# Latent attention: values stationary, two heads on one output tile, one maximum and exp over 1024 keys, output made transposed

## The chip, the cores and the metric

The kernel is one program on one core of a Trainium2 chip. Its five engines, TensorE (PE in the profile), VectorE (DVE), ScalarE (ACT), GpSimd (POOL) and SyncE (SP, which issues almost all DMAs here), work through queues of their own, each in the order in which the program was laid down, and wait for each other by semaphores. The metric is the device time of one execution in microseconds (us).

## The reference

Two transformer blocks over 1024 tokens of width 1024. The first mixes two branches on the same normed input, latent attention and a bidirectional RWKV scan, gates them, projects the sum and adds it to the input; then come a mixture of experts and a second block. The change touches latent attention alone:

```python
def attend(blk):
    qn, qr = blk
    s = (jnp.einsum('bqhd,bkhd->bhqk', qn, k_nope)
         + jnp.einsum('bqhd,bkd->bhqk', qr, k_rope))
    p = jax.nn.softmax(s.astype(jnp.float32) * scale, axis=-1).astype(v.dtype)
    return jnp.einsum('bhqk,bkhd->bqhd', p, v)
```

There are 8 heads, 64 + 32 columns for queries and keys, 64 for values, 1024 keys for each of 1024 queries, without a mask. The RWKV branch works on 4 pairs of heads: `prep` makes what needs no running state, `inverse` inverts a small triangular matrix per chunk of 64 tokens, `rwkv_chain` carries the state over 16 chunks, `finish` does the group norm.

## The kernel before

`branches` (L1964) lays down, in this order, the input projection with RWKV's work hooked into it, and then `mla` (L784), the latent attention. A list scheduler then sets the order on each engine from its own estimate of durations and from when buffers come free, so `mla` is interleaved with what is left of RWKV when the projection ends: the preps of the third and fourth head pair, `inverse` of the second to fourth, and most of the chain.

RWKV's path. `prep` (four calls per head pair; two directions, two halves) and `inverse` use memory of their own, the pool `prep`, and two PSUM banks `pw`, taken in turn. `pair(j)` lays down one prep of pair j, then `inverse(j-1)` and the chain of pair j-1, then the other three preps. `inverse` (L641) loads blocks, does 31 dependent substitution steps on VectorE (L653 and the sum behind it, ending with the copy L657), writes them out, and then joins the blocks of four units with two rounds of small products each (L671, copy L674, L676, sum L679). In a prep, L581 follows the first tanh, L583 is the scan, L608 and L609 make block diagonals, L551 is the product and L558 and L559 its masked copies. `inverse(3)` is the last user of the pool `prep`, which is then closed.

Latent attention. `mla` loads the compressed keys and queries (zk, L792; zq, L794), scales them, and makes for each pair of heads the keys and values (`keys`, L819) and for each head and half of the tokens the rotated queries (`queries`, L845). Then for each head, for each of 8 row blocks b of 128 queries and each half q of the keys:
- `score`: three float32r products into one bank S (two buffers), the row maximum on VectorE (L879), its scaling (L881), exp with a running sum on ScalarE (L883);
- `flip`: four transposes on TensorE (L889), then a copy on VectorE for q = 0 (L894), on ScalarE for q = 1 (L892);
- `values`: four products with the transposed block as the stationary operand and 64 columns of V moving (L904), 128 queries on the output partitions.

The three are one step apart: scores of step n, transposes of n-1, values of n-2. Behind a head the two halves are brought to a common maximum and divided (L930 to L938), and behind each pair the output is transposed (L943) and written (L946) to om, which the next stage, `branch_out`, reads. A float32 product is two instructions in the profile, a float32r product or a transpose one.

Memory. Pools are stacked; one that is opened on the bytes of a closed pool waits for those that used them. The tiles of `mla`'s pool take 97,728 bytes a partition, from address 18,432 to 116,160, where the projection's operands had been. The lowest tile of the pool `prep` (xn0, used by `inverse`) begins at 119,360. PSUM has eight banks, all used here: pc two, pw two, S two, pt one, pj one.

Of the kernel before, what the change touches and what calls it, by code (L numbers as in the profile page):

```python
# [7 lines left out]
F32 = mybir.dt.float32  # L8
# [31 lines left out]


def _chunks(w):
    """[..., K, N] -> [..., N/512 * K/512, 128, 2048]: chunks of 4 k-blocks by 512 columns, k fastest."""
    K, N = w.shape[-2:]
    n = w.ndim - 2
    w = w.reshape(*w.shape[:-2], K // 512, 4, 128, N // 512, 512)
    o = list(range(n)) + [n + x for x in (3, 0, 2, 1, 4)]
    return np.ascontiguousarray(w.transpose(o)).reshape(*w.shape[:n], -1, 128, 2048)


def _constants():
    """Constants of the branches, and those of the whole program."""
# [138 lines left out]
# ---------------------------------------------------------------- device program  # L191

class Prog:
# [3 lines left out]
    def consts(self, pool, temp):  # L197
        """pool: for the whole program; temp: for the branches."""
# [17 lines left out]
    def keep(self, keep, dram):  # L216
        """Scratch memory, and the small tiles that several phases use."""
# [37 lines left out]
    def slots(self, table, n, base):  # L255
        """What marks the rows in table [128, 8, n, 6]: the row of its block plus base, the block and zero."""
# [5 lines left out]
    def thirds(self, table, x):  # L262
        """x in three bfloat16 parts that add up to it exactly, to table[..., 3:6]; x is overwritten."""
# [7 lines left out]
    def iota8(self, pool):  # L271
        """The slots (from 1), each eight times."""
# [15 lines left out]
    def order(self, later, first):  # L288
        """`later` is issued behind `first` on their engine: one accumulation at a time in a bank."""
# [3 lines left out]
    def rsqrt(self, pool, out, v, n):  # L293
        """out = v ** -0.5 by Newton steps; out, v: [128, n]."""
# [16 lines left out]
    def rsqrt1(self, pool, out, v):  # L311
        """The same for one column where ScalarE has its square root at hand."""
# [9 lines left out]
def s1(P, hpool, wpool, psum):  # L322
    """Reads x, normalises it and leaves its transpose, split, in hT (hi, lo)."""
# [18 lines left out]
def z_tile(P, spool, psum, hT, m, use):  # L342
    """z^T rows of column tile m of w_in; use(s, ps): the PSUM tile of the tokens s."""
# [15 lines left out]
def phase_a(P, zpool, spool, psum, hT, after=lambda j: None):  # L359
    """z^T = (h @ w_in)^T tile by tile; what later phases need goes to scratch memory."""  # L360
# [81 lines left out]
class Rwkv:  # L442
    """The RWKV branch: a head pair (two heads on 128 partitions) and half of the tokens at a time."""
# [13 lines left out]
    def own(self, dram, pool, psw):  # L457
        """Memory for prep alone."""
# [33 lines left out]
    def stats(self, src, scale, u=None):  # L492
        """[128 (h, ch), 512] -> sums over ch per (token, head): [128 t, 8 = (block, h)] times scale."""
# [7 lines left out]
    def spread(self, st, u=None):  # L501
        """[128 t, 8 = (block, h)] -> [128 (h, ch), 512] in PSUM."""
# [8 lines left out]
    def keys(self, p, g):  # L511
        """Normalised kk of head pair p, negated, to scratch memory."""
# [12 lines left out]
    def flip(self, p, d, g, m, x):  # L525
        """x [128 (h, ch), 512 tokens], transposed per head, to part m of the scratch memory."""
# [10 lines left out]
    def diag(self, i, f):  # L537
        """Block diagonal buffer i, written by f(destination, rows) for each head."""
# [6 lines left out]
    def gram(self, lb, AR, da, mask, dr):  # L545
        """lb^T [A | R] of every chunk (partition: the index of lb), under causal masks."""
# [14 lines left out]
    def prep(self, p, d, g):  # L561
        """Chunks 8 g to 8 g + 7 of head pair p in direction d: all that needs no running state, to memory."""
# [119 lines left out]
    def finish(self, p, g, u=None):  # L682
        """Group norm, bonus and gate of head pair p; half of o_rwkv^T of the pair."""
# [33 lines left out]
def rwkv_chain(P, pool, psum, p):  # L717
    """The running states of head pair p in both directions over the chunks; leaves y^T in scratch memory."""
# [5 lines left out]
    def mm(ps, terms):  # L724
        # one accumulation group per bank: only its first product clears the bank
# [58 lines left out]
def mla(P, dram, pool, psum):  # L784
    """Latent attention; leaves o_mla^T (four tiles [128, T]) in scratch memory."""
# [9 lines left out]
    for z, w, n in ((zk, 1, 2), (zq, 0, 3)):  # L795
        for q in range(2):
# [5 lines left out]
            rb = pool.tile([128, 512], F32, name="ot", bufs=1)  # L802
# [5 lines left out]
    for q in range(2):  # L808
        s = slice(512 * q, 512 * q + 512)
        kp = pool.tile([128, 512], F32, name="ot", bufs=1)  # L810
# [6 lines left out]
    def keys(pr):  # L817
        """Keys and values of head pair pr."""
# [26 lines left out]
    def queries(h, q):  # L845
        """Rotated queries of head h, half q of the tokens."""
# [5 lines left out]
        qh, ql = (pool.tile([128, 512], F32R, name=n, bufs=2) for n in ("qh", "ql"))  # L852
# [7 lines left out]
    Vn, nq = keys(0), queries(0, 0)  # L860
    for h in range(8):
        pr, par = h // 2, h % 2
        V = Vn
        kh, kl = kt[pr % 2][par]
        if par == 0:
            O = pool.tile([128, 8, 128], F32, name="O", bufs=1)
        m = pool.tile([128, 8, 2], F32, name="m", bufs=2)
        rs = pool.tile([128, 8, 2], F32, name="rs", bufs=2)
        O2 = pool.tile([128, 8, 2, 64], F32, name="O2", bufs=1)

        def score(b, q):
            s = slice(512 * q, 512 * q + 512)
            if q == 0 and b % 4 == 0:
                qq[0] = nq
            qh, ql = qq[0]
            bs = slice(128 * (b % 4), 128 * (b % 4) + 128)
# [7 lines left out]
            return p  # L884

        def flip(p, q):
            pp = psum.tile([128, 4, 128], F32, name="pt", bufs=1)
            for k in range(4):
                nc.tensor.transpose(pp[:, k], p[:, 128 * k:128 * k + 128], P.c("ident"))  # L889
            pt = pool.tile([128, 4, 128], F32, name="pts", bufs=2)  # L890
            if q:
                nc.scalar.activation(pt, pp, AF.Copy)  # L892
            else:
                nc.vector.tensor_copy(pt, pp)  # L894
            return pt

        po = None

        def values(b, q, pt):
            nonlocal po, last  # L900
            if q == 0:
                po = psum.tile([128, 2, 64], F32, name="po", tag="pj")
            for k in range(4):
# [1131 lines left out]
```

## Time and profile before

| | us |
|---|---|
| three runs | 4285.96, 4308.72, 4307.15 |
| median | 4307.15 |
| profiled execution, first to last instruction (span) | 4303.5 |
| TensorE busy in the span | 3854.9 (90%) |
| VectorE busy | 2887.8 (67%) |
| ScalarE busy | 2145.3 (50%) |
| granted TensorE clock, mean | 0.930 |

The profile shows one execution. The span is 3.65 us below the median of the timed runs. A stretch row gives, for a part of the span, the busy time of each engine and in brackets its instructions; PEclk is the granted share of TensorE's full clock. Matmuls follow each other closer than their own duration, so what one costs is read from the spacing of starts, not from its duration.

### The profile page before, as it was taken

To read this page: it belongs to the slowest core of one execution; us is meant where nothing else is said; L and a number is where in the kernel's file an instruction comes from. 1 tells how busy PE (TensorE), PEld (TensorE's weight loads), DVE (VectorE), ACT (ScalarE), POOL (GpSimd) and SP (SyncE) were. 2 spreads that over 40 slices of the span, in tenths; PEclk is the share of its full clock that TensorE was granted. 3 is DMA by queue.
4 is the path that set the end of the run, shared out by engine and by line. 5 is a ranking of instruction groups with operands and counts; after the bars stand their busy time and mean duration, and the time that the engine had idled before them with its cause. 6 is when DMAs were issued, how large, how long until landed. Compare 5 with 4: busy or idle time off the path is not lost. (4 is left out here: it accounts for less than half of the span.)

```text
span 4303.5 us, 57981 instructions
## 1 busy us (share of the span) xinstructions
PE 3854.9 (90%) x22154; PEld 3100.3 (72%) x22154; DVE 2887.8 (67%) x4690; ACT 2145.3 (50%) x2829; POOL 418.9 (10%) x328
## 2 busy tenths in 40 slices
PE   7999988898998897999799969999969986999994
PEld 6877766776876676665679857787748875788773
DVE  4556375858557546654446758888876776788887
ACT  4322223333243224555335536777756852677774
POOL 0000000000010003333000001111010000111101
PEclk9999988988899898999899979999979997999997
DMA  3455665453435557997332359999941155899994
GB/s 106 140 169 148 182 196 161 120 153 92 150 107 173 212 193 269 317 304 227 120 132 82 131 205 338 370 376 384 373 158 69 69 202 207 304 359 377 384 373 168
DMA packets 362342, 925.00 MB, mean 215 GB/s; under 512 B 147600, under 2 KB 205712, under 8 KB 290128
## 3 DMA queue, kind: packets, MB, share of 16 engines
q1 hardware_dynamic: 343632, 870.93, 56.4%
q0 software_dynamic: 18432, 50.36, 4.7%
q8 instruction: 175, 2.87, 0.3%
q14 instruction: 103, 0.84, 0.1%
HBM read 770.68 MB, written 167.25 MB: 218 GB/s over the span
## 5 line engine op out<-in xcount | busy, mean ns | idle before, releaser
L253 DVE TENSOR_TENSOR wlo<-wraw,whi 128x2048 fp32r<-128x2048 f32 x498 | 1134.2, 2289 | 307.1 <-ACT whi L253 303.8
L253 ACT ACTIVATE whi<-wraw 128x2048 fp32r<-128x2048 f32 x498 | 955.0, 1919 | 378.3 <-PE g L286 254.0
L285 PE MATMUL g<-wlo,xth 128*128 128x512 f32 x1280 | 510.0, 398 | 6.7 <-DVE wlo L253 6.7
L284 PE MATMUL g<-whi,xth 128*128 128x512 f32 x1280 | 513.7, 402 | 2.3 <-ACT xth L253 1.6
L286 PE MATMUL g<-whi,xtl 128*128 128x512 f32 x1280 | 508.4, 397 | 7.7 <-DVE xtl L253 7.3
L286 PEld LDWEIGHTS g<-whi,xtl 128*128 128x128 f32 x1280 | 243.5, 190 | 63.7 <-DVE xtl L253 12.7
L285 PEld LDWEIGHTS g<-wlo,xth 128*128 128x128 f32 x1280 | 244.0, 191 | 61.4 <-DVE wlo L253 9.1
L284 PEld LDWEIGHTS g<-whi,xth 128*128 128x128 f32 x1280 | 244.4, 191 | 57.3 <-ACT xth L253 3.9
L284 PE MATMUL z<-hT_hi,w_hi 128*128 128x512 f32 x592 | 243.0, 411 | 9.7 <-ACT w_hi L253 6.7
L1635 POOL DMA_INDIRECT e_xg<-xm,e_ix x32 | 75.5, 2359 | 1719.5 <-DVE e_ix L1633 956.6
L285 PE MATMUL z<-hT_lo,w_hi 128*128 128x512 f32 x592 | 242.0, 409 | 0.0
L286 PE MATMUL z<-hT_hi,w_lo 128*128 128x512 f32 x592 | 241.0, 408 | 0.0
L285 PE MATMUL g<-wlo,e_hh 128*128 128x512 f32 x512 | 202.4, 398 | 15.5 <-DVE wlo L253 15.5
L284 PE MATMUL g<-whi,e_hh 128*128 128x512 f32 x512 | 204.3, 400 | 8.2 <-ACT e_hh L253 8.0
L286 PE MATMUL g<-whi,e_hl 128*128 128x512 f32 x512 | 196.5, 391 | 0.2
L904 PE MATMUL po<-V,pts 128*128 128x64 f32 x1024 | 142.5, 285 | 6.3 <-DVE tab L856 4.9
L284 PEld LDWEIGHTS z<-hT_hi,w_hi 128*128 128x128 f32 x592 | 115.2, 195 | 41.5 <-ACT w_hi L253 7.4
L904 PEld LDWEIGHTS po<-V,pts 128*128 128x128 f32 x1024 | 135.4, 204 | 12.1 <-DVE tab L856 5.2
L755 POOL TENSOR_SCALAR SW<-S,wc 128x64 f32<-128x64 f32 x120 | 65.5, 563 | 785.0 <-DVE S L773 701.3
L285 PEld LDWEIGHTS z<-hT_lo,w_hi 128*128 128x128 f32 x592 | 115.0, 194 | 30.4 <-issue 4.5
L286 PEld LDWEIGHTS z<-hT_hi,w_lo 128*128 128x128 f32 x592 | 114.4, 193 | 30.0 <-issue 3.8
L1235 PE MATMUL g<-wraw,m_hT 128*128 128x512 f32 x256 | 120.3, 610 | 13.1 <-ACT m_y L1236 8.1
(531 smaller groups left out, 8308.7 us busy)
## 6 DMA issues: line engine op xcount, KB each, us to landing
wraw<-in_w_gu SPq DMA_DIRECT2D x256, 1024.0 KB
wraw<-in_w_dn SPq DMA_DIRECT2D x128, 1024.0 KB
wraw<-in_w SPq DMA_DIRECT2D x96, 1024.0 KB
rwt<-rw SPq DMA_DIRECT2D x32, 1152.0 KB
w_raw<-in_w_in SPq DMA_DIRECT2D x37, 512.0 KB
rw<-flip SPq DMA_DIRECT2D x96, 128.0 KB
rw<-rAR SPq DMA_DIRECT2D x16, 512.0 KB
gt<-z_out SPq DMA_DIRECT2D x16, 512.0 KB
```

Of the source, the lines that this page charges most:

```text
L253: return self.nc.scalar.activation(hi, src, AF.Copy), self.nc.vector.tensor_sub(lo, src, hi.bitcast(F32))
L284: t.matmul(ps, lh, rh, start=first, stop=False)
L285: t.matmul(ps, lh, rl, start=False, stop=False)
L286: t.matmul(ps, ll, rh, start=False, stop=last)
L755: nc.gpsimd.tensor_scalar(SW[:, d], S[:, d], P.wc[:, c, 4 * d + p:4 * d + p + 1], None, op0=OP.mult)
L904: i = nc.tensor.matmul(po[:, q], pt[:, k], V[:, 4 * q + k, 64 * par:64 * par + 64], start=(k == 0), stop=(k == 3))
L1235: nc.tensor.matmul(ps, ht[:, k], w[:, k, n], start=(k == 0), stop=(k == 1))
L1635: nc.gpsimd.indirect_dma_start(out=xg, out_offset=None, in_=self.x, in_offset=bass.IndirectOffsetOnAxis(ap=ix[:, :1], axis=0))
```

## The change

- `score` now makes both halves of the keys before it looks at them: six products into one tile S of two banks, of which there is one buffer; one maximum over 1024 columns (L871), one scaling (L872), one exp (L874). The correction between halves at the end of a head is gone.
- `flip` transposes 1024 columns in two groups of four (L882), through the one bank pt, into one tile pts of which there are three buffers.
- `values` takes both heads of a pair at once: V is the stationary operand, 64 columns of it for each head, the transposed probabilities (128 columns) move; the first head's output comes on partitions 0 to 63, the second's on 64 to 127 (L896), already transposed. The reciprocals of the sums are spread over the 64 partitions of each head by two small products with the identity (L904), copied by ScalarE (L907) and multiplied on VectorE (L908). The transposes of the output are gone.
- Heads go in pairs, row block by row block: a step is one row block of one head, 64 steps in all, and values run every second step. Queries have three buffers instead of two, ot two instead of one.

The tiles of the pool now take 105,600 bytes, from 18,432 to 124,032; the last one, the third pts, lies at 119,936 to 124,032. In the rest of the file the diff takes out docstrings and comments. Its core:

```diff
-            qh, ql = (pool.tile([128, 512], F32R, name=n, bufs=2) for n in ("qh", "ql"))
+        qh, ql = (pool.tile([128, 512], F32R, name=n, bufs=3) for n in ("qh", "ql"))
...
+    def score(h, b, qs, m):
+        qh, ql = qs
+        kh, kl = kt[h // 2 % 2][h % 2]
+        bs = slice(128 * (b % 4), 128 * (b % 4) + 128)
+        S = psum.tile([128, 2, 512], F32, name="S", bufs=1)
+        for q in range(2):
             s = slice(512 * q, 512 * q + 512)
-            S = psum.tile([128, 512], F32, name="S", bufs=2)
-            P.mm3(S, qh[:, bs], ql[:, bs], kh[:, s], kl[:, s], True, True)
-            nc.vector.reduce_max(m[:, b, q:q + 1], S, axis=AX.X)
-            nm = pool.tile([128, 1], F32, name="nm", bufs=4)
-            nc.vector.tensor_scalar(nm, m[:, b, q:q + 1], -sc, None, op0=OP.mult)
-            p = pool.tile([128, 512], F32, name="p", bufs=3)
-            nc.scalar.activation(p, S, AF.Exp, bias=nm, scale=sc, accum_out=rs[:, b, q:q + 1])
+            P.mm3(S[:, q], qh[:, bs], ql[:, bs], kh[:, s], kl[:, s], True, True)
+        S = S.rearrange("p q t -> p (q t)")
+        par = h % 2
+        nc.vector.reduce_max(m[:, par:par + 1], S, axis=AX.X)
+        nc.vector.tensor_scalar(m[:, par:par + 1], m[:, par:par + 1], -sc, None, op0=OP.mult)
+        p = pool.tile([128, T], F32, name="p", bufs=2)
+        nc.scalar.activation(p, S, AF.Exp, bias=m[:, par:par + 1], scale=sc, accum_out=m[:, 2 + par:3 + par])
...
+        pt = pool.tile([128, 8, 128], F32, name="pts", bufs=3)
+        for q in range(2):
             pp = psum.tile([128, 4, 128], F32, name="pt", bufs=1)
...
+    def values(V, pts, m, out):
+        po = psum.tile([128, 2, 128], F32, name="po", tag="pj")
+        last = [None, None]
+        for k in range(8):
+            for par in range(2):
+                r = slice(64 * par, 64 * par + 64)
+                i = nc.tensor.matmul(po[r, 0], V[:, k, r], pts[par][:, k], start=(k == 0), stop=(k == 7),
+                                     skip_group_check=True)
...
+        nc.vector.reciprocal(m[:, 2:4], m[:, 2:4])
+        for par in range(2):
+            r = slice(64 * par, 64 * par + 64)
+            i = nc.tensor.matmul(po[r, 1], m[:, 2 + par:3 + par].to_broadcast([128, 64]), P.c("ident"),
+                                 start=True, stop=True, skip_group_check=True)
...
+        nc.scalar.activation(out, po[:, 1], AF.Copy)
+        nc.vector.tensor_mul(out, out, po[:, 0])
```

The change moves instructions. On SyncE's queue, the loads of zk and zq before stand among the loads of a prep of the third pair (k, nkk, r and v of `prep`, kd its output):

```order
L485 DMA k<-zr_101 128x512
L485 DMA nkk<-kn_134 128x512
L485 DMA r<-zr_100 128x512
L485 DMA v<-zr_102 128x512
L792 DMA zk<-zm_109 128x1024
L792 DMA zk<-zm_110 128x1024
L794 DMA zq<-zm_106 128x1024
L593 DMA kd_140<-t_3749 128x512
L794 DMA zq<-zm_107 128x1024
```

After the change the same loads stand on SyncE's queue behind the last loads (L665, L668) and writes (L489) of `inverse(3)`, the first loads of the fourth pair's chain (rw_131) and the first of a `finish` (y):

```order
L668 DMA xt_188<-rE_198 32x8x32 x2
L665 DMA bd_203<-rL_196 64x8x64 x2
L489 DMA rw_131<-rXT 128x4x128 x2
L745 DMA rwt<-rw_131 128x2304 x2
L485 DMA y_8091<-yd_87 128x512
L485 DMA y_8093<-yd_91 128x512
L792 DMA zk<-zm_109 128x1024
L792 DMA zk<-zm_110 128x1024
L794 DMA zq<-zm_106 128x1024
```

They have moved past four preps and two `inverse`s.

On TensorE, near the end of latent attention, two groups of scores of before stand close together, with only the transposes of the step before between them (the waits are those of the instruction, Activation being ScalarE):

```order
L284 MATMUL S<-kh_9848,qh 128x512 [waits Activation_49]
L285 MATMUL S<-kl_9849,qh 128x512
L286 MATMUL S<-kh_9848,ql 128x512
L889 MATMUL pt<-cst,p 128x128 [waits DVE_49]
L889 MATMUL pt<-cst,p 128x128 x3
L284 MATMUL S<-kh_9848,qh 128x512 [waits Activation_49]
```

After the change a step of the second half of latent attention on TensorE reads so:

```order
L284 MATMUL S<-kh_9848,qh 128x512 [waits Activation_49]
L285 MATMUL S<-kl_9849,qh 128x512
L286 MATMUL S<-kh_9848,ql 128x512
L284 MATMUL S<-kh_9848,qh 128x512
L285 MATMUL S<-kl_9849,qh 128x512
L286 MATMUL S<-kh_9848,ql 128x512
L882 MATMUL pt<-cst,p 128x128 [waits Activation_49]
L882 MATMUL pt<-cst,p 128x128 x3
L896 MATMUL po<-pts,V 64x128 x7
L904 MATMUL po<-cst,m 64x128 x2
L882 MATMUL pt<-cst,p 128x128 [waits DVE_49]
L882 MATMUL pt<-cst,p 128x128 x3
```

The wait before the first S is for the exp of the step before, since S has one buffer; before it was for the exp two steps back. On TensorE's queue the first scores stand behind nearly three quarters of the chain's products, and the last products of the chain stand in front of the 34th of the 64 steps; 17 of the chain's 64 steps lie between. Before, the chain's last products stand behind the last scores.

## Rows read from the trace of the kernel before

**Rows 1.** Stretches: length, busy PE, PEld, DVE, ACT, POOL, granted clock, DMA share, GB/s.

```profile
600.00:700.00 100.00, 73.84 (x557) 60.24 (x552) 51.71 (x100) 24.73 (x57) 10.13 (x16) 0.68 0.61 177
700.00:1360.00 660.00, 612.03 (x5926) 499.04 (x5926) 442.61 (x1146) 248.82 (x646) 51.98 (x105) 0.90 0.44 130
1360.00:1420.00 60.00, 39.26 (x249) 26.96 (x249) 39.85 (x84) 16.92 (x27) 2.01 (x4) 0.77 0.72 256
```

**Rows 2.** Single lines: count, duration ns min/median/max, first to last start us.

```profile
L792 SPq DMA_DIRECT2D zk<-zm x2: 429/430/432, 602.9 to 603.4; - x2
...
L284 PE MATMUL S<-kh,qh x128: 389/478/799, 698.4 to 1346.4; 128*128 128x512 f32 x128
...
L946 SPq DMA_DIRECT2D om<-ot x8: 319/362/401, 902.8 to 1368.9; - x8
```

**Rows 3.** VectorE in order of time, RWKV's path: start, us, line, operation.

```profile
315.39 0.16 DVE L653 TENSOR_TENSOR rXp<-rX,rLd 128x1 f32<-128x1 f32 x1 [0.23 <-DMA rLd<-rL]
...
376.06 1.11 DVE L657 COPY rLd<-rX 128x1024 f32<-128x1024 f32 x1
...
618.24 1.06 DVE L657 COPY rLd<-rX 128x1024 f32<-128x1024 f32 x1
...
710.49 0.42 DVE L581 TENSOR_SCALAR t<-t 128x512 f32<-128x512 f32 x1
...
740.70 0.43 DVE L581 TENSOR_SCALAR t<-t 128x512 f32<-128x512 f32 x1 [3.38 <-ACT t L580]
...
760.53 0.42 DVE L559 TENSOR_TENSOR rMB<-pw,cstb 128x256 f32<-128x256 f32 x1
...
1075.35 1.11 DVE L657 COPY rLd<-rX 128x1024 f32<-128x1024 f32 x1
...
1101.65 0.42 DVE L674 COPY bd<-pw 64x256 f32<-64x256 f32 x1 [5.21 <-PE pw L671]
1108.48 0.42 DVE L679 TENSOR_TENSOR rXT<-pw,xt 128x256 f32<-128x256 f32 x1 [0.54 <-PE pw L676]
...
1131.24 0.42 DVE L679 TENSOR_TENSOR rXT<-pw,xt 128x256 f32<-128x256 f32 x1 [1.66 <-PE pw L676]
```

**Rows 4.** Groups of instructions from 690 to 1390 us: busy us, mean ns, idle before.

```profile
L883 ACT ACTIVATE p<-S,nm 128x512 f32<-128x512 f32 x128 | 87.6, 686 | 80.9 <-DVE nm L881 70.9 <-PE pt L889 4.4 <-DVE rs_t L307 1.9
L879 DVE TENSOR_REDUCE m<-S 128x1 f32<-128x512 f32 x128 | 87.2, 687 | 33.0 <-PE S L286 32.0
...
L894 DVE COPY pts<-pt 128x512 f32<-128x512 f32 x64 | 43.9, 686 | 10.9 <-PE pt L889 9.7 <-PE po L904 0.5
...
L883 ACT ACTIVATION_READ_ACCUMULATOR p<-S,nm 128x1 f32 x128 | 25.0, 196 | 0.0
...
L881 DVE TENSOR_SCALAR nm<-m 128x1 f32<-128x1 f32 x128 | 18.1, 146 | 1.8
...
L253 ACT ACTIVATE whi<-wraw 128x2048 fp32r<-128x2048 f32 x2 | 3.8, 1902 | 3.4 <-DMA wraw<-in_w_br 3.4
```

**Rows 5.** TensorE in order of time: start, us, line, operation, count in the row.

```profile
1150.05 1.10 PE L904 MATMUL po<-V,pts 128*128 128x64 f32 x8
1150.99 0.61 PE L889 MATMUL pt<-cst,p 128*128 128x128 f32 x4
...
1151.67 0.40 PE L285 MATMUL S<-kl,qh 128*128 128x512 f32 x1
1151.90 0.39 PE L286 MATMUL S<-kh,ql 128*128 128x512 f32 x1
...
1154.40 2.84 PE L855 MATMUL pj<-zq,wq 128*128 128x512 f32 x6
...
1222.81 0.40 PE L732 MATMUL pc<-rwt 64*64 64x64 f32 x8
1223.04 0.40 PE L732 MATMUL pc<-U,rwt 64*64 64x64 f32 x8
1223.37 2.05 PE L838 MATMUL pj<-wv,zk 128*128 128x128 f32 x16
```

More of the change, by code (lines that the diff above doesn't have):

```diff
@@ L801, in mla @@
                                     P.c("ident"))
-            rb = pool.tile([128, 512], F32, name="ot", bufs=1)
+            rb = pool.tile([128, 512], F32, name="ot", bufs=2)
             nc.scalar.activation(rb, ps.rearrange("p b t -> p (b t)"), AF.Copy)
@@ L809, in mla @@
         s = slice(512 * q, 512 * q + 512)
-        kp = pool.tile([128, 512], F32, name="ot", bufs=1)
+        kp = pool.tile([128, 512], F32, name="ot", bufs=2)
         nc.sync.dma_start(kp, P.zm[5][:, s])
@@ new lines, in score @@
+    def score(h, b, qs, m):
[4 more added lines that the diff above has]
+        for q in range(2):
+            s = slice(512 * q, 512 * q + 512)
+            P.mm3(S[:, q], qh[:, bs], ql[:, bs], kh[:, s], kl[:, s], True, True)
[5 more added lines that the diff above has]
+        nc.scalar.activation(p, S, AF.Exp, bias=m[:, par:par + 1], scale=sc, accum_out=m[:, 2 + par:3 + par])
+        return p
@@ L887, in flip @@
+    def flip(p):
+        pt = pool.tile([128, 8, 128], F32, name="pts", bufs=3)
+        for q in range(2):
             pp = psum.tile([128, 4, 128], F32, name="pt", bufs=1)
             for k in range(4):
-                nc.tensor.transpose(pp[:, k], p[:, 128 * k:128 * k + 128], P.c("ident"))
-            pt = pool.tile([128, 4, 128], F32, name="pts", bufs=2)
+                nc.tensor.transpose(pp[:, k], p[:, 128 * (4 * q + k):128 * (4 * q + k) + 128], P.c("ident"))
             if q:
-                nc.scalar.activation(pt, pp, AF.Copy)
+                nc.scalar.activation(pt[:, 4:8], pp, AF.Copy)
@@ L893, in flip @@
             else:
[L894 to L903, printed above, removed]
-                i = nc.tensor.matmul(po[:, q], pt[:, k], V[:, 4 * q + k, 64 * par:64 * par + 64],
-                                     start=(k == 0), stop=(k == 3))
-                if q and k == 0:
-                    P.order(i, last)
-                last = i
-            if q:
-                nc.vector.tensor_copy(O2[:, b], po)
@@ L912, in mla @@
-        last = None
-        qq = [None]
-        todo = [(b, q) for b in range(8) for q in range(2)]
-        ps_, pts = {}, {}
-        for n in range(len(todo) + 2):
-            if n < len(todo):
-                ps_[n] = score(*todo[n])
-            if 0 <= n - 1 < len(todo):
-                pts[n - 1] = flip(ps_.pop(n - 1), todo[n - 1][1])
-            if n >= 2:
-                values(*todo[n - 2], pts.pop(n - 2))
-            if n == 4:
-                nq = queries(h, 1)
-            if n == 12 and h < 7:
-                if par:
-                    Vn = keys(pr + 1)
-                nq = queries(h + 1, 0)
@@ L938, in mla @@
-        nc.vector.tensor_add(O[:, :, 64 * par:64 * par + 64], O2[:, :, 0], O2[:, :, 1])
-        if par:
-            for g in range(2):
-                pp = psum.tile([128, 4, 128], F32, name="pj", tag="pj")
-                for k in range(4):
-                    nc.tensor.transpose(pp[:, k], O[:, 4 * g + k], P.c("ident"))
-                ot = pool.tile([128, 512], F32, name="ot", bufs=1)
-                nc.scalar.activation(ot, pp.rearrange("p a t -> p (a t)"), AF.Copy)
-                nc.sync.dma_start(P.om[pr][:, 512 * g:512 * g + 512], ot)
+                nc.vector.tensor_copy(pt[:, 0:4], pp)
@@ new lines, in flip @@
+        return pt
+    def values(V, pts, m, out):
[6 more added lines that the diff above has]
+                                     skip_group_check=True)
+                if k:
+                    P.order(i, last[par])
+                last[par] = i
+        nc.vector.reciprocal(m[:, 2:4], m[:, 2:4])
[3 more added lines that the diff above has]
+                                 start=True, stop=True, skip_group_check=True)
+            P.order(i, last[par])
+        nc.scalar.activation(out, po[:, 1], AF.Copy)
+        nc.vector.tensor_mul(out, out, po[:, 0])
@@ new lines, in mla @@
+    todo = [(pr, b, par) for pr in range(4) for b in range(8) for par in range(2)]
+    Vs, qs = {0: keys(0)}, {(h, 0): queries(h, 0) for h in range(2)}
+    ps_, pts, ms, ots = {}, {}, {}, {}
+    for n in range(len(todo) + 2):
+        if n < len(todo):
+            pr, b, par = todo[n]
+            if par == 0:
+                ms[pr, b] = pool.tile([128, 4], F32, name="m", bufs=4)
+            h = 2 * pr + par
+            ps_[n] = score(h, b, qs[h, b // 4], ms[pr, b])
+            if b % 4 == 3:
+                del qs[h, b // 4]
+        if 0 <= n - 1 < len(todo):
+            pts[n - 1] = flip(ps_.pop(n - 1))
+        if n >= 2 and n % 2:
+            pr, b, _ = todo[n - 2]
+            if b % 4 == 0:
+                ots[pr] = pool.tile([128, 512], F32, name="ot", bufs=2)
+            values(Vs[pr], (pts.pop(n - 3), pts.pop(n - 2)), ms.pop((pr, b)),
+                   ots[pr][:, 128 * (b % 4):128 * (b % 4) + 128])
+            if b % 4 == 3:
+                nc.sync.dma_start(P.om[pr][:, 512 * (b // 4):512 * (b // 4) + 512], ots.pop(pr))
+        if n < len(todo):
+            pr, b, par = todo[n]
+            if b == 2:
+                qs[2 * pr + par, 1] = queries(2 * pr + par, 1)
+            if b == 6 and pr < 3:
+                if par == 0:
+                    Vs[pr + 1] = keys(pr + 1)
+                qs[2 * pr + 2 + par, 0] = queries(2 * pr + 2 + par, 0)
```

26 lines of the change are left out of this document (removed).

## Prediction

> **What bounds the kernel now.** I read first the stretch table of the profile, to find the part of the span that the change lives in; then who starts and ends the latent attention; then the path that the other branch takes beside it; last the durations and spacings of the single instructions. The reader should see in the stretch table [rows 1] that from 700 to 1360 us TensorE is busy for 612 of 660 us at a mean granted clock of 0.90: two branches are interleaved, latent attention and the tail of RWKV, and each fills the other's waits. Before it (600 to 700) and behind it (1360 to 1420) it is busy for 74 and 65% and the clock stands at 0.68 and 0.77. Latent attention runs from its loads at 602.9 and its first scores at 698.4 to the last write of its output at 1368.9 [rows 2]. That end, together with the end of the RWKV chain just behind it, is what the rest of the program waits for, so the question is when latent attention ends after the change.
>
> **The start moves.** Nothing in the diff says so, but the order does: on SyncE's queue the loads of zk and zq stood among the loads for the third head pair's prep, and now stand behind the last loads and writes of `inverse(3)`. The pool of latent attention has grown over the lower end of prep's memory. So the first part of the stretch, in which the two branches covered each other, is left to RWKV alone. How long does RWKV need alone? Its path there is serial. From the end of the substitution of `inverse(1)` at 618.24 + 1.06 = 619.3 [rows 3] it has to go through three rounds of joining products (call one U), six preps that nothing else covers (P) and two substitutions (I; one prep lies inside one of them).
> - U: beside latent attention, from 1075.35 + 1.11 to 1131.24 + 0.42 is 55 us [rows 3]. The fastest of its four rounds takes 7.25 from copy to sum (1101.65 to 1108.48 + 0.42), four of them 29, and writing out and loading come on top. Bounds 30 and 55; I take 44.
> - P: beside latent attention one prep follows the other after 30.2 us (710.49 to 740.70). From there to its last masked product one takes 20.3 (740.70 to 760.53 + 0.42). Bounds 20 and 30; I take 24.
> - I: the first one ran where latent attention had not begun, from 315.39 to 376.06 + 1.11, 61.8 us; I take that.
>
> Sum 3 x 44 + 6 x 24 + 2 x 61.8 = 400, so RWKV reaches that point at 1019; at best 90 + 120 + 124 = 334 (953); at worst it is no faster than before, 1132. From the loads to the first scores lie two waits for loads, ten scalings, two queries and one set of keys; before it was 95 us among full queues, I take 30 (20 to 60). First scores: 1049 instead of 698.
>
> **What latent attention then takes.** Per head and row block there were two rounds of 512 keys, now there is one of 1024. The score tile S was two buffers of one bank; now it is one buffer of two banks, and TensorE's order shows the first score product of each step waiting for ScalarE, that is for the exp of the step before. So one step is a closed loop [rows 4, 5]:
> - six score products: five spacings of 0.23 and 0.39 for the last, 1.54;
> - the maximum over 1024: 0.687 for 512 columns, 0.146 for VectorE's operation on one, so 0.54 more for 512 more, 1.23;
> - VectorE's order in the changed kernel puts the copy of the transposed block between the maximum and its scaling: 0.686 and 0.146;
> - exp over 1024: between 0.686 for 512 and 1.902 for 2048, 1.09; reading the sum 0.196; three handovers, 0.1.
>
> That is 5.0 us; 64 steps are 320. TensorE itself needs less in a step: scores 1.4, eight transposes 0.9, eight value products. These 512 products of two instructions each took 0.118 an instruction (eight in 0.94, 1150.05 to 1150.99): 121 us in all [rows 5]. Now 128 columns move past 64 stationary ones. No row has that shape. With 128 stationary columns it is 0.128 (16 in 2.05), and two halves of the array at once would make it 0.064. For the halves speak the chain's 64x64 products, eight in 0.23 (1222.81 to 1223.04) [rows 5]. Bounds 66 and 131 us, with 8 to 16 for the products that spread the reciprocals; I take the halves as side by side. The gain of about 50 us on TensorE is real but lies inside a loop that does not wait for it: 1.4 + 0.9 + 1.0 + 0.1 = 3.4 of 5.0 us.
> The Trainium skill, "Perfetto Trace Analysis", Optimizing Tensor Performance, Matmuls, says that independent groups of matmuls should rotate through banks, so that emptying one overlaps the next; the change takes this rotation from the scores. The kernel before, which has it, keeps TensorE 93% busy here, as that rule would have it; without the loop the time would be that of the third rival below.
>
> On top come, in TensorE's queue, what also has to be issued behind the first scores: 14 queries of 2.84 (six instructions of 0.47), three sets of keys of 8 x 0.47 + 32 x 0.128 = 7.9, and, counted in the order, 17 chain steps of 64 instructions at 0.03, 1.9 each: 95 us, against 64 x 1.6 = 102 idle. In a queue in order about half will land where the scores could have gone: 48 (0 to 95). The clock: at two thirds busy TensorE will be granted full speed only part of the time, as between 600 and 700 [rows 1]. I take a mean of 0.8, so four steps in ten have their scores at the lower level, 1.2 instead of 2.4 GHz: 64 x 0.4 x 1.5 = 38 (0 to 60). Changing between whole and divided array: from the last chain group to the next 128x128 product 0.33 instead of 0.23 (1223.04 to 1223.37), so 0.10 each way; twice two changes for each of 32 value groups are 13, half of them in the loop, 6.
> The Trainium skill, "TensorEngine Tiling (Array Packing)", Tiling Modes, Key Properties, says that a change of mode drains the engine and that tiles work independently; the rows bear out both, the drain at 0.10 us, and only the second decides anything here.
>
> Sum 320 + 48 + 38 + 6 = 412 (350 to 500). End of latent attention: 1049 + 412 = 1461 instead of 1369, +92. Behind it something comes back: RWKV's last group norms, which before ran between 1360 and 1420 with TensorE idle for 21 of 60 us, are then long done: -20 (0 to -30). Net +72. The sum is made against the profiled execution, 4303.5 us; the median of the three runs is 4307.15, 3.7 more, which I leave as it is: 4303.5 + 72 + 3.7 = 4379.
>
> **Rivals.**
> 1. *RWKV alone is quick and the gap closes* (the other side). Its preps and joins fall to their lower bounds, and scores begin at 953 + 20 = 973; the additions hide, 350. End 1323, -46, with the tail -66: 4241. It decides from scores that begin before 1369 + 20 - 412 = 977 with my loop, or before 1039 with 350. For it: VectorE had only 443 of 660 us there. Against: the chain's products will run cold, and the joins wait for DMA. 0.11.
> 2. *The halves do not run side by side.* Then each step has 1.0 us more on TensorE behind the transposes, and 64 steps add 64 us: 4443. For it: no row has this shape. Against: the chain's products. 0.15.
> 3. *The loop costs nothing*, because what is queued fills it and TensorE stays the bound: 64 x 3.4 + 95 + 6 = 319, end 1368, with the tail -21: 4286; with some of the loop showing it is no change. 0.11.
> 4. *RWKV is no faster alone*: it was held by DMA and its own order. Then the start is 1132 + 30, +113 on the sum: 4492. 0.07.
>
> **How the numbers follow.** The forecast has 0.56. About 0.5% or 21 us is what a measurement of this kernel can tell from no change. The forecast and rivals 2 and 4 are slower (0.78); rival 1 is faster, rival 3 is shared between faster and the same: faster 0.13, same 0.09. The bounds of the forecast alone (first scores 973 to 1162, 350 to 500) reach from 4241 to 4580; to hold eight in ten with the rivals I give 4285 to 4505.
>
> **What would show it.** The loads of zk near 1020 and not 603; the first scores near 1050; from there to the end of the chain TensorE full, behind it a repeating step of 5 to 6 us in which the score products wait for ScalarE and the clock falls below 0.9; value products at about 0.06 an instruction; the last write of the output near 1460; RWKV's group norms over by then. If zk is loaded near 950 or sooner, or the steps without the chain last under 4.5 us, the forecast is wrong; if they last over 6.5, rival 2 or a colder clock.

## The result, and the profile after

The changed kernel takes 4414.49 us (median of 4 runs, 4407.48 to 4418.30); the kernel before, run beside it on the same chip, 4304.61. The ratio is 1.027 (95% interval 1.025 to 1.029): slower by 110 us, 35 more than the 4379 that were forecast, and inside the range. The profiled execution has a span of 4413.3 us, 109.8 more than before.

The stretch table of the changed kernel, columns as in [rows 1]; the first three rows are the stretches of [rows 1] again:

```profile
600.00:700.00 100.00, 73.18 (x636) 61.79 (x636) 46.38 (x97) 21.16 (x52) 9.51 (x18) 0.62 0.55 156
700.00:1360.00 660.00, 512.31 (x5170) 397.96 (x5170) 385.43 (x911) 188.33 (x450) 58.51 (x106) 0.76 0.47 142
1360.00:1420.00 60.00, 49.55 (x339) 35.63 (x340) 31.81 (x68) 23.76 (x44) 0.00 (x0) 1.00 0.25 85
...
700.00:900.00 200.00, 128.67 (x1342) 108.40 (x1344) 115.54 (x267) 41.73 (x111) 22.85 (x38) 0.62 0.59 167
...
900.00:1100.00 200.00, 131.56 (x1312) 108.64 (x1309) 113.79 (x274) 39.56 (x105) 19.31 (x34) 0.60 0.52 160
...
1200.00:1300.00 100.00, 98.61 (x1059) 72.10 (x1058) 57.08 (x132) 40.57 (x91) 7.71 (x16) 1.00 0.32 105
...
1400.00:1500.00 100.00, 83.91 (x591) 60.09 (x589) 43.52 (x80) 37.45 (x70) 0.00 (x0) 0.98 0.06 18
```

TensorE does 512 us of work from 700 to 1360 instead of 612. From 700 to 1100 it is busy for two thirds of the time at a granted clock of 0.60 to 0.62, near the lower of its two levels (1.2 of 2.4 GHz); from 1100 to 1500 it is busy for 84 to 99 of each 100 us at 0.98 to 1.00. The stretch that two branches shared has become two stretches, one behind the other. The lines that start and end latent attention (count, ns, first to last start) say the same, against [rows 2]:

```profile
L792 SPq DMA_DIRECT2D zk<-zm x2: 442/540/639, 1047.9 to 1048.4; - x2
...
L284 PE MATMUL S<-kh,qh x128: 387/475/799, 1108.5 to 1515.1; 128*128 128x512 f32 x128
...
L931 SPq DMA_DIRECT2D om<-ot x8: 319/323/327, 1174.5 to 1526.2; - x8
```

The loads come 445 us later, the first scores 410, and the last output is written at 1526.2 instead of 1368.9, 157 later. The work itself takes 418 us instead of 670. Of the 157, 47 come back behind it.

### The profile page after: what moved, and what is told of

It is laid out like the page before. It is cut to its first block, busy times and chain, and to the rows that moved or that the text cites. A ratio compares the mean times of both kernels' runs of the same rounds, so it can differ in the third digit from the quotient of the medians.

```text
span 4413.3 us, 57846 instructions
## 1 busy us (share of the span) xinstructions
PE 3854.2 (87%) x22250; PEld 3079.9 (70%) x22250; DVE 2864.0 (65%) x4498; ACT 2131.0 (48%) x2717; POOL 423.2 (10%) x328
## 3 DMA queue, kind: packets, MB, share of 16 engines
q0 software_dynamic: 18432, 50.36, 4.5%
## 5 line engine op out<-in xcount | busy, mean ns | idle before, releaser
L871 DVE TENSOR_REDUCE m<-S 128x1 f32<-128x1024 f32 x64 | 78.3, 1224 | 82.1 <-PE S L286 81.8
L285 PEld LDWEIGHTS g<-wlo,e_hh 128*128 128x128 f32 x512 | 96.4, 188 | 43.1 <-DVE wlo L253 25.2
```

What stands on the lines that cost most here:

```text
L285: t.matmul(ps, lh, rl, start=False, stop=False)
L871: nc.vector.reduce_max(m[:, par:par + 1], S, axis=AX.X)
```

## Experiments

Each was timed in four to nine runs beside the kernel before, whose median lay between 4299 and 4305 from one occasion to the next; differences between two rows of the table are therefore good to a few us. "om" is the last write of latent attention's output and "yd" that of the RWKV chain, from the profiled execution of each, as is the span (us).

| kernel | time | ratio to before (95%) | first scores | om | yd | span |
|---|---|---|---|---|---|---|
| before | 4305 | | 698 | 1368.9 | 1382.9 | 4303.5 |
| changed | 4414 | 1.027 (1.025 to 1.029) | 1108 | 1526.2 | 1321.2 | 4413.3 |
| e_fit | 4247 | 0.988 (0.986 to 0.990) | 700 | 1263.4 | 1325.5 | 4244.3 |
| e_fit64 | 4411 | 1.026 (1.025 to 1.028) | 1097 | 1515.3 | 1323.4 | 4404.4 |
| e_pad | 4433 | 1.031 (1.028 to 1.033) | 1099 | 1544.5 | 1304.8 | 4431.0 |
| e_fit_oldval | 4281 | 0.996 (0.994 to 0.998) | 697 | 1315.1 | 1362.1 | 4279.9 |
| e_fit2 | 4255 | 0.990 (0.988 to 0.991) | 697 | 1275.5 | 1337.4 | 4249.3 |
| e_ctl | 4410 | 1.026 (1.025 to 1.028) | 1099 | 1511.3 | 1329.2 | 4398.7 |
| e_s2 | 4393 | 1.021 (1.019 to 1.024) | 1122 | 1505.3 | 1339.1 | 4396.8 |
| e_pt2 | 4427 | 1.029 (1.028 to 1.031) | 1114 | 1531.1 | 1343.7 | 4424.5 |
| e_nm | 4395 | 1.021 (1.020 to 1.023) | 1105 | 1509.3 | 1316.4 | 4399.3 |
| e_fit_nm | 4256 | 0.989 (0.988 to 0.991) | 696 | 1277.9 | 1341.0 | 4252.3 |
| e_warm | 4400 | 1.023 (1.022 to 1.025) | 1087 | 1516.2 | 1309.5 | 4403.1 |

### Is it the memory? e_fit, e_fit64, e_pad

e_fit, the changed kernel made to fit under prep's memory (all three places where ot is taken are changed alike):

```
-            rb = pool.tile([128, 512], F32, name="ot", bufs=2)
+            rb = pool.tile([128, 512], F32, name="ot", bufs=1)
...
-        wk = pool.tile([128, 2, 128], F32, name="wk")
-        wv = pool.tile([128, 2, 128], F32, name="wv")
+        wk = pool.tile([128, 2, 128], F32, name="wk", bufs=1)
+        wv = pool.tile([128, 2, 128], F32, name="wk", bufs=1)
...
-        wq = pool.tile([128, 3, 128], F32, name="wq", bufs=2)
+        wq = pool.tile([128, 3, 128], F32, name="wq", bufs=1)
...
-                ms[pr, b] = pool.tile([128, 4], F32, name="m", bufs=4)
+                ms[pr, b] = pool.tile([128, 4], F32, name="m", bufs=2)
```

> The changed kernel with its pool made 4,672 bytes smaller (ot, wq and the weights of the keys one buffer each, two instead of four small m), so that it ends at 119,360 and no longer lies on the memory of prep. Theory A (what costs the 110 us is the late start; the loop of one step is hidden when RWKV runs beside it): zk is loaded near 603 and first scores come near 700 as before, TensorE is the bound from 700 to 1360 again with about 40 to 60 us less work, the last write of om comes at 1310 to 1370 and the time is 4250 to 4305. Theory B (the closed loop of scores, maximum and exp costs by itself, wherever it stands): the first scores come near 700 too, but the 64 steps stretch over more than 700 us beside RWKV, the last write comes later than 1400, and the time is 4340 or more. Theory C (the single buffers that make room cost as much as the start gains): the first scores near 700, with idle time in front of the products of queries and keys that wait for DMA; 4310 to 4400.

e_fit64 is e_fit with the last line undone, 64 bytes:

> The shrunk kernel (4247 us) with four instead of two buffers of the small tile m, 64 bytes in all: the pool now ends at 119,424, 64 bytes over the lowest tile of prep. Nothing else differs. Theory A (the overlap with prep's memory holds back everything in the pool, whatever its size): zk is loaded near 1048 again and the time is that of the changed kernel within 1%, 4380 to 4440. Theory B (the shrunk kernel is fast because of something else in the trims, or the wait grows with the bytes that overlap, and only the tile that overlaps waits): 4240 to 4300.

e_pad is the kernel before with one line more at the head of `mla`:

```
+    pool.tile([128, 1968], F32, name="pad")
```

> The kernel before with one unused tile of 7,872 bytes at the front of latent attention's pool, so that the pool ends at 124,032 as in the changed kernel; no instruction is added. Theory A (late start is the cost): zk is loaded near 1048, the first scores come near 1105; the old steps alone are bounded by TensorE, 64 x 4.2 + 95 = 364 us and more, so the last om write comes at 1465 to 1530, and with a tail that is some 40 us shorter the time is 4350 to 4420, nearly that of the changed kernel. Theory B (the new loop is the cost): under 4325, since nothing of the old computation changes.

The lines of e_fit (zk, scores, om, and the RWKV chain's yd), behind them the one of e_fit64, and last those of e_pad (zk and om):

```profile
L792 SPq DMA_DIRECT2D zk<-zm x2: 430/431/432, 607.1 to 607.5; - x2
...
L284 PE MATMUL S<-kh,qh x128: 387/476/799, 700.2 to 1249.3; 128*128 128x512 f32 x128
...
L931 SPq DMA_DIRECT2D om<-ot x8: 319/320/343, 785.8 to 1263.4; - x8
...
L780 SPq DMA_DIRECT2D yd<-Y x64: 319/422/1282, 491.1 to 1325.5; - x64
```

```profile
L792 SPq DMA_DIRECT2D zk<-zm x2: 436/584/732, 1045.5 to 1046.0; - x2
```

```profile
L793 SPq DMA_DIRECT2D zk<-zm x2: 440/570/700, 1047.9 to 1048.4; - x2
...
L947 SPq DMA_DIRECT2D om<-ot x8: 319/326/327, 1242.9 to 1544.5; - x8
```

Fitting the pool makes the changed kernel 1.2% faster than the one before, and 64 bytes over the border take all of it back: 164 us between two kernels that differ in two small buffers. zk lies far below prep's memory and waits all the same, so the wait holds back the whole pool, not the tile that overlaps. e_pad shows it without the change: no instruction added, and the kernel before loses 133 us. Theory A holds in all three, if not to the last figure: e_fit came out 3 us below its range (its last om write, at 1263, 47 before the range), e_pad 13 above. The lost overlap is the whole loss, and the new computation itself is a gain: 53 us where it starts early (4247 against 4300), about 20 where it starts late (4414 against 4433, timed on different occasions).

### What is the gain? e_fit_oldval

```
+        po = psum.tile([128, 64], F32, name="po", tag="pj")
+        for k in range(8):
+            nc.tensor.matmul(po, pt[:, k], V[:, k, 64 * par:64 * par + 64], start=(k == 0), stop=(k == 7))
+        nc.vector.reciprocal(m[:, 2 + par:3 + par], m[:, 2 + par:3 + par])
+        nc.vector.tensor_scalar(out, po, m[:, 2 + par:3 + par], None, op0=OP.mult)
...
+                        nc.tensor.transpose(pp[:, 128 * c:128 * c + 128], O[:, 4 * g + c], P.c("ident"))
```

> The shrunk kernel (pool ends at 119,360), but with the value products of the kernel before: transposed probabilities stationary, 64 columns of V moving, one head at a time with 128 queries on the output partitions, the row scaled by the reciprocal on VectorE, and the output transposed behind each pair of heads. One maximum and exp over 1024 keys stay. If the value products side by side are worth what they save on TensorE (512 x 2 instructions of 0.118 against 0.064 us, 55 us, less 16 for the spreading products, plus the transposes of the output), and TensorE is the bound from 700 to 1360: 30 to 50 us slower than the shrunk kernel. If something else is the bound there (the loop, or RWKV's path): within 10 us of it.

34 us slower than e_fit, as expected: the values side by side are worth about 34 of the 53, the single maximum and exp (with what goes with them) the other 19. The split is not exact, since e_fit_oldval also has two buffers of pts instead of three, which no run separates. They count here because TensorE is nearly full in e_fit:

```profile
700.00:1260.00 560.00, 525.15 (x5636) 395.01 (x5634) 386.39 (x872) 224.98 (x510) 47.58 (x96) 0.97 0.47 140
```

### What ends last when it starts early? e_fit2, e_fit_nm

In e_fit, om is written 105.5 us sooner than before, yet the span is only 59.2 shorter. The RWKV chain's end, 57.4 sooner, is now the later one. Two more kernels change latent attention's own work there. e_fit2 makes room in another way (pts with two buffers, values ahead of the transposes):

```
...
-        pt = pool.tile([128, 8, 128], F32, name="pts", bufs=3)
+        pt = pool.tile([128, 8, 128], F32, name="pts", bufs=2)
...
+        if 0 <= n - 1 < len(todo):
+            pts[n - 1] = flip(ps_.pop(n - 1))
```

> Another way to fit: pts with two buffers, the values laid down ahead of the transposes of their step, wk and wv in one buffer, two small m; ot and wq keep two buffers, and the pool ends at 118,848. Theory A (where latent attention has room beside RWKV, RWKV's path is what ends last, as in the shrunk kernel, where om is written at 1263 and the last yd at 1325): within 12 us of 4247. Theory B (the single buffers of ot and wq cost something there): 12 to 40 us faster. Theory C (two pts stop the transposes while values are read, and latent attention becomes the end): 15 us or more slower.

e_fit_nm adds to e_fit the order on VectorE that e_nm, below, adds to the changed kernel.

> The shrunk kernel (4247 us) with the same order on VectorE. Theory A (there the RWKV chain's end, 1325, is what is late, not latent attention, 1263): within 12 us of 4247, whatever a step of latent attention does. Theory B (latent attention still holds back RWKV through what it keeps waiting): 12 to 40 us faster.

Both stay within 9 us of e_fit, a difference hardly clear of the spread of the runs, so theory A holds in both by its number. But neither made latent attention end sooner: om comes 12 and 15 us later than in e_fit, the chain's end 12 and 16, so a shorter latent attention was not tested here. What speaks for the chain is the spacing to the end: in all kernels that start early (before among them) the span is the chain's end plus 2911 to 2921 us, while its distance from om varies from 2935 to 2981; in all that start late it is the end of om plus 2886 to 2894. The end that sets the time has changed sides.

### What sets a step when latent attention is alone? e_ctl, e_s2, e_nm, e_pt2

e_s2 gives S a second buffer; its two banks are those of the fourth pair's chain, which moves to the banks of the other chains. e_ctl moves that chain alone, without the last pair of lines.

```
-                R.big, pc3 = p("fin"), p("pc3", space=PS)
-                rwkv_chain(P, p("ch3"), pc3, 3)
+                R.big = p("fin")
+                rwkv_chain(P, p("ch3"), pc, 3)
...
-        S = psum.tile([128, 2, 512], F32, name="S", bufs=1)
+        S = psum.tile([128, 2, 512], F32, name="S", bufs=2)
```

> The changed kernel with two buffers of the two-bank score tile S; the two banks come from the fourth head pair's chain, which now uses the two banks of the other chains. The start stays late. Theory A (the loop through the one S buffer sets the length of the steps once latent attention is alone): first scores near 1108 as in the changed kernel; the step falls from 5.8 to about 4 us, where TensorE is the bound (3.4 us and a share of queries and keys), latent attention takes 300 to 350 instead of 418 us, and the time is 4310 to 4350. Theory B (the step is set by TensorE's order or by VectorE and ScalarE together, not by the buffer): no gain, 4390 to 4430, with scores that come earlier and wait later.

> The changed kernel with the fourth pair's chain in the PSUM banks of the other chains, and one buffer of S as it was: what the run with two buffers of S (4393 us) changed beside S. If sharing these banks is harmless, 4405 to 4425, and the second S buffer alone is worth the 20 us. If sharing delays the chain or the group norms, 4425 to 4450, and the second S buffer is worth 35 to 55 us, as the shortening of latent attention (418 to 383 us) would have it.

e_nm takes VectorE's copy out of the loop:

```
+        P.scaled = nc.vector.tensor_scalar(m[:, par:par + 1], m[:, par:par + 1], -sc, None, op0=OP.mult)
...
+                P.order(nc.vector.tensor_copy(pt[:, 0:4], pp), P.scaled)
```

> The changed kernel with one order added on VectorE: the copy of the transposed block (0.68 us) goes behind the scaling of the maximum, not between the maximum and its scaling. The start stays late. Theory A (a step is the closed loop through the single S tile, and the copy is one of its links): steps where nothing else runs fall from 5.0 to 5.2 us to 4.3 to 4.6, latent attention from 418 to 375 to 395 us, the time is 4370 to 4392. Theory B (the copy frees the bank pt, so that what the maximum gains the second group of transposes loses): steps stay at 5.0, the time is 4400 to 4420.

The changed kernel near its end, where nothing else runs, in order of time (start, us, engine, line, operation):

```profile
1500.61 1.22 DVE L871 TENSOR_REDUCE m<-S 128x1 f32<-128x1024 f32 x1 [1.55 <-PE S L286]
1501.76 0.68 DVE L886 COPY pts<-pt 128x512 f32<-128x512 f32 x1
1502.35 0.14 DVE L872 TENSOR_SCALAR m<-m 128x1 f32<-128x1 f32 x1
...
1502.61 1.12 ACT L874 ACTIVATE p<-S,m 128x1024 f32<-128x1024 f32 x1 [3.26 <-DVE m L872]
...
1503.08 1.09 PE L896 MATMUL po<-pts,V 128*64 128x128 f32 x16
...
1504.10 0.50 PE L284 MATMUL S<-kh,qh 128*128 128x512 f32 x1
...
1505.81 1.22 DVE L871 TENSOR_REDUCE m<-S 128x1 f32<-128x1024 f32 x1 [3.32 <-PE S L286]
```

This has the links of the loop that was forecast: maximum, copy, scaling, exp, then the next scores, 5.2 us from maximum to maximum. But in this step the exp is not the last thing that the scores wait for: it ends at 1503.73, and they start at 1504.10, straight behind 16 instructions of value products, which stand behind the second transposes. In the step before, where most of the value products come earlier, the scores do wait for the exp:

```profile
1497.66 1.11 ACT L874 ACTIVATE p<-S,m 128x1024 f32<-128x1024 f32 x1
...
1498.92 0.50 PE L284 MATMUL S<-kh,qh 128*128 128x512 f32 x1 [0.34 <-ACT p L874]
```

The two kinds of step alternate, and the last seven take 4.9 to 5.2. In e_nm:

```profile
1485.55 1.23 DVE L871 TENSOR_REDUCE m<-S 128x1 f32<-128x1024 f32 x1 [1.25 <-PE S L286]
...
1486.81 0.15 DVE L872 TENSOR_SCALAR m<-m 128x1 f32<-128x1 f32 x1
1486.88 0.68 DVE L886 COPY pts<-pt 128x512 f32<-128x512 f32 x1
1487.08 1.11 ACT L874 ACTIVATE p<-S,m 128x1024 f32<-128x1024 f32 x1 [2.62 <-DVE m L872]
...
1488.20 1.09 PE L896 MATMUL po<-pts,V 128*64 128x128 f32 x16
...
1489.22 0.50 PE L284 MATMUL S<-kh,qh 128*128 128x512 f32 x1
...
1490.92 1.23 DVE L871 TENSOR_REDUCE m<-S 128x1 f32<-128x1024 f32 x1 [3.36 <-PE S L286]
```

The copy has left the loop, and exp starts 1.5 instead of 2.0 us behind the maximum. But the second transposes wait for that copy, the 16 instructions of value products come behind them, and the scores stand behind those: the step takes 5.4. The other kind of step, with most of the value products elsewhere, takes 4.5 (1481.07 to 1485.55 in the same view). So half of what theory A of e_nm expected came: 19 us, with latent attention at 404, and the time lies between the two ranges. A second S is worth about 17 us (4393 against 4410 of e_ctl), with latent attention 29 us shorter (412 to 383) and begun 23 later. TensorE is then nearly full from the first scores on:

```profile
1122.00:1500.00 378.00, 365.93 (x3239) 263.20 (x3238) 224.77 (x501) 158.77 (x325) 12.78 (x28) 1.00 0.27 86
```

Of the two theories for e_s2, A named the gain but not its size, B the time but not the gain: the loop costs about 20 us, not the 60 to 100 of theory A, because TensorE's own work is close behind it. The Trainium skill ("Perfetto Trace Analysis", Optimizing Tensor Performance, Matmuls) says that independent groups of matmuls should rotate through different banks. Here that is worth these 17 us.

e_pt2, the two free banks given to pt and pj, each with two buffers, in place of S:

```
...
-            pp = psum.tile([128, 4, 128], F32, name="pt", bufs=1)
+            pp = psum.tile([128, 4, 128], F32, name="pt", bufs=2)
...
```

> As the control above (one buffer of S, the fourth chain in the shared banks), but the two free banks go to a second buffer of pt and a second one of pj. If the loop scores, maximum, exp through the one S tile alone sets a step: within 10 us of the control, steps still 5.0 to 5.2 where nothing else runs. If the ring of transposes and copies through the one bank pt (and keys, queries and values through the one bank pj) holds the steps as much as S does: 15 to 40 us faster than the control, most of it at the pair boundaries, where a step now lasts 11 to 18 us.

Neither came: 17 us slower than e_ctl. The steps at the pair boundaries, 12 to 16 us in e_ctl, did fall to 5 to 6, but the mean of the others grew from 5.9 to 6.5, and the first scores came 15 us later. More buffers gave the scheduler another order, and what this order cost is not taken apart, so the run says nothing certain on the ring through pt.

### Was RWKV alone held back by the clock? e_warm

```
+    for _ in range(45):
+        W = psum.tile([128, 2, 512], F32, name="S", bufs=1)
+        for k in range(20):
+            nc.tensor.matmul(W[:, 0, 0:128], P.c("ident"), P.c("ident"), start=True, stop=True)
```

> The changed kernel with 900 products of the identity by itself into the idle tile S, laid down ahead of latent attention, which fill TensorE's idle time between the end of the projection and the loads of zk, while RWKV runs alone. The result does not use them. Each costs about 0.23 us at full clock. Theory A (RWKV alone was slower than forecast, 426 instead of 400 us, because its products ran at a granted clock of 0.6): the granted clock from 650 to 1040 rises above 0.9, the four joins fall below 45 us, zk is loaded 20 to 60 us sooner than 1048, and the time is 4355 to 4395. Theory B (RWKV alone is a chain of VectorE, handovers and DMA waits, and the clock matters little): zk within 12 us of 1048, time 4400 to 4430. If the added products get in RWKV's way: later than 1060, over 4425.

A stretch of e_warm, columns as above (the changed kernel has 0.62 there), and its loads:

```profile
700.00:900.00 200.00, 192.73 (x2104) 174.66 (x2103) 117.81 (x266) 39.84 (x102) 17.91 (x32) 0.99 0.56 159
```

```profile
L796 SPq DMA_DIRECT2D zk<-zm x2: 447/458/470, 1033.6 to 1034.1; - x2
```

From 700 to 900 the granted clock rises from 0.62 to 0.99, over the whole stretch from 650 to 1040 from 0.60 to 0.96; zk comes 14 us sooner, with 15 us in the time. That is between the theories and nearer to B: with TensorE at 1.6 times the mean clock, 14 us come off the stretch. The joins did not fall below 45 us; they took 51, 41 and 55. The run has a cost of its own, though: at times the added products (L792) stand in front of RWKV's on TensorE. In the third join ScalarE had written its operand of L676 by 1002.7, and L676 began at 1007.4, behind 24 instructions of the added products and 16 of the chain:

```profile
1001.58 5.26 PE L792 MATMUL S<-cst 128*128 128x128 f32 x24
...
1002.32 0.38 ACT L672 ACTIVATE bd<-pw 64x256 f32<-64x256 f32 x1 [0.41 <-DVE bd L674]
...
1007.38 1.97 PE L676 MATMUL pw<-xt,bd 128*128 128x32 f32 x16
```

So the 14 us are what the clock gave back less what these products cost, and how much of RWKV's time alone is due to the clock stays open.

## Why the prediction was right, and where its sizes were off

**The start moves: right.** The growth of the pool, found from the order and the addresses, is the cause; e_fit, e_fit64 and e_pad show it.

**RWKV alone: 423 us instead of 400.** VectorE's path in the changed kernel, in order of time, against [rows 3]:

```profile
621.19 1.04 DVE L657 COPY rLd<-rX 128x1024 f32<-128x1024 f32 x1
...
675.13 0.42 DVE L679 TENSOR_TENSOR rXT<-pw,xt 128x256 f32<-128x256 f32 x1 [2.88 <-PE pw L676]
...
756.05 0.16 DVE L653 TENSOR_TENSOR rXp<-rX,rLd 128x1 f32<-128x1 f32 x1 [2.63 <-DMA k<-zr]
...
815.21 1.03 DVE L657 COPY rLd<-rX 128x1024 f32<-128x1024 f32 x1
...
861.06 0.42 DVE L679 TENSOR_TENSOR rXT<-pw,xt 128x256 f32<-128x256 f32 x1 [2.88 <-PE pw L676]
...
948.20 0.16 DVE L653 TENSOR_TENSOR rXp<-rX,rLd 128x1 f32<-128x1 f32 x1 [3.04 <-DMA y<-yd]
...
999.08 1.03 DVE L657 COPY rLd<-rX 128x1024 f32<-128x1024 f32 x1
...
1044.67 0.42 DVE L679 TENSOR_TENSOR rXT<-pw,xt 128x256 f32<-128x256 f32 x1 [3.41 <-PE pw L676]
```

From the end of a copy L657 to the end of the fourth sum L679 the joins took 53, 45 and 45 us (forecast 44 each), the substitutions 60 and 52 (62), and what lies between, three preps each time, 80 and 87, so 28 a prep (24). The end stood in its bounds, 1045 instead of 1019; the preps are the term that was too small (167 for 144), the joins are 12 over, the substitutions 12 under; the start was 3 us later. The clock, which the estimate had left out, is worth 14 us or more there by e_warm.

**The lead: 63 us instead of 30**, from RWKV's end at 1045.1 to the first scores, and so just outside the forecast's own bounds of 20 to 60. The estimate counted two waits for loads, scalings, queries and keys. It left out the 16 instructions that split the rotary keys (eight each on ScalarE and VectorE, some 5 us in a row) and SyncE's queue: the last load of zq is issued at 1064.8 and that of the rotary keys at 1072.3, among the loads of RWKV's group norms.

**Latent attention: 418 us instead of 412, by terms that were not right one by one.** The durations stood, against [rows 4] (groups: busy us, mean ns, idle before):

```profile
L871 DVE TENSOR_REDUCE m<-S 128x1 f32<-128x1024 f32 x64 | 78.3, 1224 | 82.1 <-PE S L286 81.8
L874 ACT ACTIVATE p<-S,m 128x1024 f32<-128x1024 f32 x64 | 71.2, 1112 | 54.6 <-DVE m L872 44.6 <-DVE U L739 3.8 <-DVE hst L694 2.9
...
L886 DVE COPY pts<-pt 128x512 f32<-128x512 f32 x64 | 43.8, 685 | 10.0 <-PE pt L882 8.4 <-PE po L896 1.3
```

The forecast had 1.23 and 1.09 for the first two, and 5.0 for the step. 63 steps at 5.0 are 315; they took 403 (first maximum 1112.85, last 1515.96), 88 more. The forecast had 48 for queued work, 6 for changes of mode and 38 for the clock. The clock cost next to nothing: it was granted at 0.98 to 1.00 up to 1500, with TensorE busy for 84 to 99% and not for the two thirds that the forecast's clock rested on. Most of the 88 must then be queued work that stands in front of the scores; that much is read from the trace and not tested. 31 of it show at the three pair boundaries, whose steps last 18.3, 16.7 and 11.3 us. The forecast had counted 95 us of queued work and left out the products of RWKV's group norms, which are laid down there too: 36 instructions of 512 columns (L688, L708, L712), 17 us at the forecast's own 0.47. That half would hide was a guess, and the clock, a second wrong term, balanced it.

The loop, too, was given too much weight. The forecast made it the ruling term, 320 of 412, and put the time without it at 319 (its third rival). With the second buffer of S, e_s2 took 383 us for latent attention, at a TensorE busy for 366 of 378 us and at full clock. So TensorE's own work was a limit close behind the loop, the forecast's sum for it was about 60 us too small, and opening the loop is worth about 20. That the parts came within 6 us of the 418 is luck.

**Values side by side: right.** 16 instructions in 1.02 us (1503.08 to 1504.10 above), 0.064 each, as taken; rival 2 falls. That the loop does not wait for them holds for one kind of step only; in the other the scores stand behind them, as shown above. No run takes this gain out where the start is late. Where it starts early, TensorE is the bound and the gain shows: about 34 us. The prediction did not ask what the change would do with the overlap kept.

**The tail: -47 instead of -20.** Before, the last om write was not the last thing waited for: the chain ended 14 us behind it, the first split of the outputs came 22 us behind it (1391.2) and the last 100 us later (1491.5), since RWKV's group norms were late (last one written at 1456.3). After the change these are 7 us (1533.2) and 77 us (1610.5), which is 38 of the 47; the rest is not traced. The 20 counted only TensorE's idle time between 1360 and 1420.

So the span of 4413.3 instead of 4375.5 (4303.5 + 72) is: start 59 later (1108 for 1049), latent attention 6 longer, tail 27 shorter, 38 in all. Rival 1 needed scores before 977, rival 3 a loop that costs nothing and scores that take 319 us, rival 4 an RWKV no faster alone (it ended 87 us sooner): none came.

## What to carry to other kernels

Before a change adds a buffer, look at where its pool ends: 64 bytes over the border of memory that another stage still holds can delay everything in the pool, and here cost three times what the new computation gains. A new computation is judged only with the overlap kept; and when it then gets shorter, look for the branch that ends last next, since 105 us saved on one branch gave 59.

## What had not been expected of the hardware

- Raising TensorE's mean granted clock from 0.60 to 0.96 over a stretch of 390 us, by added products that themselves stand in RWKV's way at times, shortened a serial path of products, copies and DMA by 14 us only (e_warm).
- In the changed kernel TensorE kept a granted clock of 0.98 and more from 1100 to 1500, through steps in which it waits for ScalarE; the forecast had 0.8.
- A second buffer for two PSUM tiles made the kernel 17 us slower (e_pt2 against e_ctl); the order of the instructions changed with it, and which part of that cost the time is open.
